# A transformer layer in float32 on one core: the down projection's first activations loaded in two turns, more weight sums made ahead, and matmuls of ones at the start

## The chip, the core and the metric

The kernel runs on one core of one Trainium2 chip. A core has five engines that follow their own instruction streams in order and wait for one another through semaphores: TensorE (PE, matrix products into PSUM banks), VectorE (DVE), ScalarE (ACT), GpSimd (POOL) and SyncE (SP). Tiles lie in SBUF with 128 partitions. DMA transfers are issued by SP, ACT or POOL and carried by 16 DMA engines.

The metric is the device time of one execution in microseconds (us).

## What is computed

One layer of an encoder for 512 tokens of width 2048, in float32. Cut to what matters:

```python
h  = rmsnorm(x, norm_mix)
qa, ka, va, qb, kb, vb, ga, gb = split(h @ w_in)        # 2048 x 8704
A  = window_attention(rope(rmsnorm(qa)), rope(rmsnorm(ka)), va, sink)   # 8 heads
B  = neighbourhood_attention(rmsnorm(qb), rmsnorm(kb), vb, rpb)         # 8 heads
merged = sigmoid(ga) * (A @ w_branch_a) + sigmoid(gb) * (B @ w_branch_b)
x  = x + merged @ w_out
h2 = rmsnorm(x, norm_ffn)
u  = depthwise_conv3(h2 @ w_up)                         # 2048 x 11264
gate, val = split(u)
x  = x + (silu(gate) * val) @ w_down                    # 5632 x 2048
```

## The kernel before

**Number format.** Activations are kept transposed (features on partitions, tokens in the free dimension). Every float32 operand is split in two halves of the rounded format fp32r, a high half by a cast on ACT and a low half by a subtraction on DVE, and every product is three matmuls: high by high, high by low, low by high. In the attention stage and the first gates the weights are split at L163 (`hi`) and L164 (`lo`); later at L645 (`wh`) and L646 (`wl`), or at L746 and L747 for weights that are multiplied as they are. Everything on PE is issued at L78.

**Stages.** First the projections of q, k and v with the heads of both attentions. The work of the heads is cut in pieces that wait in `queue`; each weight unit takes some of them along (`run_queued`, with raised priority). Where nothing is said to the contrary a scheduler sorts the instructions by a simulated timeline of its own; what is issued through `keep` or `dma` keeps the order of the program on its engine. Then the gates: `gates(0)` and `gates(4)` are two blocks of 512 columns in plain products (8 units of 1024x128 weights each, 96 matmuls of 128x512, 4 banks); at their end `gate_to_slot` multiplies the four banks on DVE (L848), applies the sigmoid on ACT (L849) and stores on POOL's queue (L854). The banks tagged `mm` are four, so the next block starts when L848 has emptied them. `gates(8)` ends the attention, and it loads x again and forms h for what follows. The heads that are still queued run beside the first gates: scores into `tr` banks, bias and mask on DVE (L531, L534), maximum (L477), exponential and scaling on ACT (L494), transposes on PE (L503), their split on ACT (L507) and DVE (L508), products with v on PE, and a copy of the output on ACT (L519).

**Products by sums.** From gate block 3 on a unit of weights is a 2x2 arrangement of blocks and is multiplied by seven products instead of eight, which needs sums of the weights' blocks (three DVE instructions for each unit, L600, L603, L604) and sums of the activations' blocks (`forms`). `combine` joins the seven banks (first an ACT copy, L799). The sums of some units are `kept`: made far ahead by `make_early`, while the unit counter `u` lies in one of the `windows`. For each such unit POOL loads two tiles of 256 KB (L614, `s<-in_w_up`), DVE adds four times one unit later (L620), and ACT's queue stores two tiles of 256 KB (`sums<-s`, L629) two units after that. When the unit's turn comes, SP loads one tile of 512 KB (`f<-sums`) in the place of one of 128 KB and the three sums. SBUF has 56 tiles of 128x512, `slot()`, for this and for all else.

**Down.** The 22 `up` steps leave `act` in DRAM: for each pair of 256 features eight blocks (four values and four sums, 128 KB each, seven blocks in the last part). `down(part, n)` multiplies three parts of 7, 7 and 8 pairs by four column blocks. `load_act` loads a pair's blocks on SP's queue, into one half of a slot each, and `split_act` splits them in place, each with an ACT cast (L1075) and a DVE subtraction (L1076) of 128x256. Part 0's pairs are loaded in the last `up` step and split from there on; those of parts 1 and 2 in the step ahead of their own. Steps (0,0), (0,3) and (1,3) use no sums: 48 matmuls of 128x256 a unit, of the four value blocks only (`tiles_by_halves`: tiles 0, 7, 1 and 6 of a pair). All other steps have 42 matmuls of 128x256 a unit.

**Start.** SP's queue loads `gmix` and then x and the first weights; POOL fills a tile `ones`, used at L276.

Of the kernel before, what the change touches and what calls it, by code (L numbers as in the profile page):

```python
# [11 lines left out]
F32 = mybir.dt.float32  # L12
F32R = mybir.dt.float32r
# [5 lines left out]
P = 128  # L19
# [20 lines left out]
def trunk_kernel(  # L40
# [6 lines left out]
    nc = tc.nc  # L47
# [32 lines left out]


    gmix = const.tile([P, KD], F32, tag="gmix", name="gmix")
    dma(gmix, norm_mix)
    warm = const.tile([P, 1], F32, tag="warm", name="warm")
    nc.vector.memset(warm, 0.0)
    nc.scalar.activation(warm, warm, AF.Square)
    ident = const.tile([P, P], F32, tag="ident", name="ident")
    make_identity(nc, ident)
    mhalf = const.tile([P, 16], F32, tag="mhalf", name="mhalf")
    nc.gpsimd.memset(mhalf, -0.5)  # L90
    ones = const.tile([P, P], F32, tag="ones", name="ones")
    nc.gpsimd.memset(ones, 1.0)
    nsink = const.tile([P, 8], F32, tag="nsink", name="nsink")
    n_kept = sum(width for _, width in KEPT)
    smalls = const.tile([P, n_kept], F32, tag="smalls", name="smalls")
# [473 lines left out]


    ffn, early, fetched, added, windows = {}, deque(), deque(), deque(), []
    keep = tc.keep_in_program_order

    class Product:

# [389 lines left out]
        nc.vector.tensor_tensor(r, r, s, ALU.add)  # L965
        merged[m] = split(r)

    windows.append((9, len(units)))
    for blk in range(2):
        gates(blk * 4, gate_to_slot)  # L970
    gates(8, gate_to_quad, pre=pre_forms, before=before_forms, post=post_forms)
    for blk in range(3, 8):
        gate_products(
# [85 lines left out]
    wait = lambda: None  # L1059
    unfinished = deque([wait, wait, wait])  # L1060

    def load_act(part, n):

        if 0 <= n < len(parts[part]):
            blocks = (0, 2, 7, 5, 4, 6, 3, 1)[:8 - (part == 2)]
            tiles = [slot(F32R) for _ in blocks]
            for o, i in zip(tiles, blocks):
                dma(o[:, 256:].bitcast(F32), act[parts[part][n]][:, i])
            acts[part].append(tiles)

    def split_act(part, n):
        if 0 <= n < len(parts[part]):
            for o in acts[part][n]:
                hi, lo = o[:, :256], o[:, 256:]
                keep(nc.scalar.copy(hi, lo.bitcast(F32)))  # L1075
                keep(nc.vector.tensor_tensor(  # L1076
                    lo, lo.bitcast(F32), hi.bitcast(F32), ALU.subtract))

    def up(s):
        def evac(gate, val):  # L1080
            g, v = Conv(gate, 2 * s), Conv(val, 44 + 2 * s)
            made = []

            def silu():
                keep(nc.scalar.activation(g.o, g.o, AF.Silu))

            def out_part():
                keep(nc.vector.tensor_tensor(v.o, g.o, v.o, ALU.mult))
                made.extend(form_sums(v.o))
# [12 lines left out]
        def before(i):  # L1102
            if s == 0 and i in (0, 2, 4):
                form_pair(5 + i // 2)
            if s == 0 and i == 4:
                rows["f"] = row_factor("f")
            if s == 0 and i == 7:
                rows["f"] = rows["f"]()[1]
            if s == pairs_ff - 1:
                load_act(0, i - 1)  # L1110

        def after(i):
            if s == pairs_ff - 1:
                split_act(0, i - 6)

        view = w_up.rearrange("(d b p) (h n) -> d p b h n", b=2, p=P, h=2)
        products(view[:, :, :, :, s * 256:(s + 1) * 256], range(KD // 2), h2, evac,
                 before=before, after=after, kept=(2, 3, 7) if s else range(8))

    def down(part, n):  # L1120
        held = []

        def before(i):
            if n == 0 and part:
                load_act(part, 6 + i)
            if part == n == 0 and i == 4:
                run_queued(1)
            if part == 0 and n == 1 and i == 1:
                queue.extend(unfinished)
            if part < 2 and n == 3:  # L1130
                load_act(part + 1, i - 1)
            if part == 2 and i == 4:
                for j in range(2):
                    held.append(quad("ao"[j]))
                    dma(held[j], total[2 * n + j])

        def after(i):
            if n == 0:
                split_act(part, i + (5 if part else 2))
            if part < 2 and n == 3:  # L1140
                split_act(part + 1, i - 2)

# [19 lines left out]
        else:  # L1162
            view = w_down.rearrange("(d b p) (s h n) -> s d p b h n", b=2, p=P, s=4, h=2)
            products(view[n], parts[part], acts[part], evac if part < 2 else evac_total,
                     before=before, after=after, kept=(0, 1) if part and n == 0 else (),
                     total=held if part == 2 else None)

    for s in range(pairs_ff):
# [70 lines left out]
```

## Time and profile before

| | |
|---|---|
| median of 3 executions | 2466.04 us (2465.09 to 2468.15) |
| the profiled execution | 2465.89 us |
| its span, first to last instruction | 2464.1 us |
| mean granted TensorE clock | 0.998 |
| PE, busy share of the span | 99% |
| DVE | 77% |
| ACT | 52% |
| POOL | 13% |

The chain of work that ended last lies with PE for 94% of the span, DVE 2%, DMA 1%, ACT 1%. Times below are us from the start of the span. A row of the timeline has the start, the length, the engine, the line, the operation, output<-input, the shape and the number of instructions, and in brackets the idle time before it with what ended it. A row of the windows has the stretch, its length, and for PE, PEld (weight load), DVE, ACT and POOL the busy us and the number of instructions, then the granted clock of PE, the busy share of the DMA engines and GB/s.

### The profile page before, as it was taken

The page shows a single profiled execution, that of the slowest core. Times are in us where ns is not written, and L with a number is a line of the kernel's source. Part 1 is how long each engine was busy: PE and PEld are TensorE (multiplying, and loading weights), DVE is VectorE, ACT ScalarE, POOL GpSimd, SP SyncE. Part 2 cuts the span into 40 slices and gives each one's busy share as a digit, 9 for nine tenths or more (in the row PEclk, how much of TensorE's full clock was granted, in tenths as well). Part 3 has the DMA queues.
Part 4 walks back from the last instruction along what each step waited for, and adds up shares of the span by engine and source line. Part 5 has one row for each costly group of instructions (what it writes and reads, how often), then busy time and mean ns, then how long its engine had stood idle before and what let it go on. Part 6 is the DMA issues. An engine that isn't in the chain of part 4 may idle for free.

```text
span 2464.1 us, 45745 instructions
## 1 busy us (share of the span) xinstructions
PE 2436.6 (99%) x17430; PEld 2276.2 (92%) x17430; DVE 1899.6 (77%) x3003; ACT 1283.5 (52%) x1962; POOL 330.5 (13%) x406
## 2 busy tenths in 40 slices
PE   9999999999999999999999999999999999999998
PEld 7888888888999888888999999999999999999998
DVE  6787667655888656557888888888888878696898
ACT  5354554365644322334666666666666666453633
POOL 1322122301000111111011111110111101000000
PEclk9999999999999999999999999999999999999999
DMA  5766766746655677777588888888888897766754
GB/s 197 257 230 213 234 207 230 238 139 205 197 163 175 200 271 245 237 232 245 166 213 230 224 225 224 218 234 222 224 228 218 234 277 187 218 187 176 221 158 131
DMA packets 340700, 525.45 MB, mean 213 GB/s; under 512 B 30720, under 2 KB 234112, under 8 KB 340480
## 3 DMA queue, kind: packets, MB, share of 16 engines
q1 hardware_dynamic: 254656, 319.68, 41.8%
q0 software_dynamic: 48384, 128.91, 21.8%
q10 hardware_dynamic: 37440, 73.94, 7.8%
q8 instruction: 136, 2.23, 0.4%
q14 instruction: 84, 0.69, 0.1%
HBM read 377.80 MB, written 98.57 MB: 193 GB/s over the span
## 4 chain that ended last, share of the span: by engine, by line
PE 94%; DVE 2%; DMA 1%; ACT 1%; issue 1%; SPq 0%; DVEq 0%; ACTq 0%
PE mm L78 91%; PE tr L78 2%; PE tr L503 1%; PE tr L351 0%; DVE wl L646 0%; DVE s L1076 0%; DMA a<-in_x_t 0%; DMA s<-act 0%; DMA f<-in_w_down 0%; ACT wh L645 0%; DVE u L795 0%; DVE s L687 0%; ACT s L1075 0%; DMA sums<-s 0%; DVE s L620 0%
## 5 line engine op out<-in xcount | busy, mean ns | idle before, releaser
L78 PE MATMUL mm<-s,wh 128*128 128x256 f32 (+1 forms) x9620 | 1725.0, 289 | 6.6 <-ACT wh L645 2.5
L78 PEld LDWEIGHTS mm<-s,wh 128*128 128x128 f32 x9620 | 1437.1, 188 | 48.7 <-ACT wh L645 3.1
L78 PE MATMUL mm<-s,wl 128*128 128x256 f32 (+1 forms) x4810 | 1249.9, 289 | 3.5 <-DVE wl L646 3.5
L78 PEld LDWEIGHTS mm<-s,wl 128*128 128x128 f32 x4810 | 851.0, 188 | 24.7 <-DVE wl L646 4.5
L645 ACT CAST wh<-f 128x1024 fp32r<-128x1024 f32 (+1 forms) x566 | 516.9, 942 | 482.5 <-PE mm L78 331.3
L646 DVE TENSOR_TENSOR wl<-f,wh 128x1024 fp32r<-128x1024 f32 (+1 forms) x566 | 601.8, 1088 | 147.7 <-ACT wh L645 146.3
L78 PE MATMUL mm<-hi,s 128*128 128x512 f32 x896 | 284.9, 394 | 5.7 <-ACT hi L163 5.7
L747 DVE TENSOR_TENSOR wl<-f,wh 128x1024 fp32r<-128x1024 f32 x85 | 104.1, 1224 | 165.4 <-ACT wh L746 159.7
L746 ACT CAST wh<-f 128x1024 fp32r<-128x1024 f32 x85 | 89.4, 1052 | 238.8 <-PE mm L78 207.0
L78 PEld LDWEIGHTS mm<-hi,s 128*128 128x128 f32 x896 | 167.6, 189 | 38.4 <-ACT hi L163 5.7
L163 ACT CAST hi<-raw 128x1024 fp32r<-128x1024 f32 (+1 forms) x97 | 100.9, 1040 | 188.5 <-PE mm L78 153.9
L78 PE MATMUL mm<-s,hi 128*128 128x512 f32 x640 | 195.4, 392 | 2.1 <-ACT o L519 1.6
L164 DVE TENSOR_TENSOR lo<-raw,hi 128x1024 fp32r<-128x1024 f32 (+1 forms) x97 | 117.5, 1211 | 102.8 <-ACT hi L163 98.7
L78 PE MATMUL mm<-lo,s 128*128 128x512 f32 x448 | 176.3, 395 | 0.0
L78 PEld LDWEIGHTS mm<-s,hi 128*128 128x128 f32 x640 | 119.2, 188 | 25.9 <-ACT o L519 1.8
L600 DVE TENSOR_TENSOR f<-f 128x512 f32<-128x512 f32 x195 | 133.5, 685 | 0.0
L1045 POOL DMA_DIRECT2D o<-a x44 | 52.9, 1202 | 557.8 <-ACT a L1044 336.9
L78 PE MATMUL mm<-s,lo 128*128 128x512 f32 x320 | 118.8, 391 | 0.0
L620 DVE TENSOR_TENSOR s<-s 128x256 f32<-128x256 f32 x236 | 93.2, 419 | 17.1 <-DMA s<-in_w_up 15.0
L78 PEld LDWEIGHTS mm<-lo,s 128*128 128x128 f32 x448 | 84.4, 188 | 16.6
L1042 ACT ACTIVATE o<-u,smalls 128x512 f32<-128x512 f32 x88 | 71.2, 809 | 33.3 <-DVE t L677 30.1
L603 DVE TENSOR_TENSOR f<-f 128x256 f32<-128x256 f32 x195 | 83.0, 426 | 6.7
(150 smaller groups left out, 2029.5 us busy)
## 6 DMA issues: line engine op xcount, KB each, us to landing
f<-sums SPq DMA_DIRECT2D x88, 512.0 KB, 5.3
f<-in_w_up SPq DMA_DIRECT2D x176, 256.0 KB, 3.8
o<-a POOLq DMA_DIRECT2D x88, 511.0 KB, 7.4
f<-in_w_up SPq DMA_DIRECT2D x281, 128.0 KB, 3.8
raw<-in_w_in SPq DMA_DIRECT2D x63, 512.0 KB, 4.4
sums<-s ACTq DMA_DIRECT2D x118, 256.0 KB, 4.1
s<-in_w_up POOLq DMA_DIRECT2D x86, 256.0 KB, 5.4
s<-act SPq DMA_DIRECT2D x168, 128.0 KB, 4.2
```

The lines of the kernel that those rows point to most:

```text
L78: return nc.tensor.matmul(o, l, r, start=start, stop=stop, skip_group_check=True).ins
L163: nc.scalar.copy(hi[:, c:c + n], self.raw[:, c:c + n])
L164: nc.vector.tensor_tensor(lo[:, c:c + n], self.raw[:, c:c + n], hi[:, c:c + n].bitcast(F32), ALU.subtract)
L600: keep(nc.vector.tensor_tensor(f[:, 3:5], f[:, 2::-2], f[:, 6].unsqueeze(1).to_broadcast([P, 2, 256]), ALU.add))
L603: keep(nc.vector.tensor_tensor(f[:, 5], f[:, 4], f[:, 2], ALU.add))
L620: add = lambda *args: keep(nc.vector.tensor_tensor(*args, ALU.add))
L645: keep(nc.scalar.copy(hi, f))
L646: keep(nc.vector.tensor_tensor(lo, f, hi.bitcast(F32), ALU.subtract))
L746: keep(nc.scalar.copy(hi, self.f))
L747: keep(nc.vector.tensor_tensor(lo, self.f, hi.bitcast(F32), ALU.subtract))
L1042: keep(nc.scalar.activation(self.o[:, m], u[:, m], AF.Identity, bias=cb[:, i:i + 1], scale=cw[:, i, 1:2]))
L1045: keep(nc.gpsimd.dma_start(self.o[:, :, 1:], first[:, :, :S - 1], accum_op=ALU.add))
```

## The change

Four edits:

1. At the start `gmix` is loaded on ACT's queue, `ones` is filled on DVE, and ten matmuls of ones by ones (128x128, float32) go to a bank that nobody reads.
2. The first window for early sums ends at `gates(8)` and no longer at `gates(0)`: it is 16 units longer.
3. `load_act` and `split_act` take a list of blocks. Part 0's values are loaded and split in the last `up` step and the beginning of (0,0), its sums in (0,0), and they are split there and in (0,1).
4. At (1,0) and (2,0) units 0 to 4 have kept sums in the place of units 0 and 1.

```diff
-    dma(gmix, norm_mix)
+    keep = tc.keep_in_program_order
+    keep(nc.scalar.dma_start(gmix, norm_mix))
...
+    ones = const.tile([P, P], F32, tag="ones", name="ones")
+    nc.vector.memset(ones, 1.0)
+    busy = bank("tr")
+    for _ in range(10):
+        keep(nc.tensor.matmul(busy[:, :P], ones, ones, start=True, stop=True))
...
-    windows.append((9, len(units)))
     for blk in range(2):
         gates(blk * 4, gate_to_slot)
+    windows.append((9, len(units)))
...
-    def load_act(part, n):
+    BLOCKS, VALUES, SUMS = (0, 2, 7, 5, 4, 6, 3, 1), (0, 1, 6, 7), (2, 3, 4, 5)
+
+    def load_act(part, n, which=None):
         if 0 <= n < len(parts[part]):
...
+            if n == len(acts[part]):
+                acts[part].append([None] * 8)
+            for i in which or range(8 - (part == 2)):
+                acts[part][n][i] = slot(F32R)
+                dma(acts[part][n][i][:, 256:].bitcast(F32), act[parts[part][n]][:, BLOCKS[i]])
...
             if s == pairs_ff - 1:
-                load_act(0, i - 1)
+                load_act(0, i - 2, VALUES)
...
             if s == pairs_ff - 1:
-                split_act(0, i - 6)
+                split_act(0, i - 6, VALUES)
...
             if n == 0 and part:
                 load_act(part, 6 + i)
+            if part == n == 0:
+                load_act(0, 6 + i, VALUES)
+                load_act(0, i, SUMS)
...
-            if n == 0:
-                split_act(part, i + (5 if part else 2))
+            if n == 0 and part:
+                split_act(part, i + 5)
+            if part == n == 0:
+                split_act(0, i + 2, VALUES)
+                split_act(0, i - 2, SUMS)
+            if part == 0 and n == 1:
+                split_act(0, i + 5, SUMS)
...
-                     before=before, after=after, kept=(0, 1) if part and n == 0 else (),
+                     before=before, after=after, kept=range(5) if part and n == 0 else (),
```

In number: 97 units are kept after the change, 91 before. Of the 91 the windows had room for 88, among them of the down units only unit 0 of (1,0). The first window now makes 75 units' sums in the place of 59, the second 22 in the place of 29, and all 97 are made.

**PE between the first two blocks of gates.** A row is a line and an operation with output<-input and shape, "x" the number in a row. `mm` are the banks of the gates (and `s,hi` and `s,lo` their operands), `tr` those of the heads: `tr<-s` are scores, `tr<-ident,p` transposes, `tr<-ph,s` and `tr<-pl,s` products with v. Before, in the middle of the second block:

```order
L78 MATMUL mm<-s,hi 128x512 x2
L78 MATMUL tr<-ph,s 128x256
L78 MATMUL mm<-s,lo 128x512
L78 MATMUL mm<-s,hi 128x512
L78 MATMUL tr<-s 128x256 x6
L78 MATMUL tr<-pl,s 128x256
L78 MATMUL tr<-ph,s 128x256 x2
L78 MATMUL tr<-pl,s 128x256
L78 MATMUL tr<-ph,s 128x256
L78 MATMUL mm<-s,hi 128x512
L78 MATMUL mm<-s,lo 128x512
```

After the change, from the last matmul of the first block:

```order
L78 MATMUL mm<-s,lo 128x512
L78 MATMUL tr<-s 128x256 x12
L507 MATMUL tr<-ident,p 128x128 x2
L78 MATMUL tr<-ph,s 128x2x128
L507 MATMUL tr<-ident,p 128x128 x4
L78 MATMUL tr<-pl,s 128x2x128
L78 MATMUL tr<-ph,s 128x2x128
L78 MATMUL tr<-ph,s 128x256
L507 MATMUL tr<-ident,p 128x128 x2
L78 MATMUL tr<-s 128x256 x3
```

The rows after these go on in the same way: 84 instructions of the heads (56 matmuls 256 wide and 28 transposes; line numbers are 3 to 5 higher in the changed kernel) stand in one piece between the two blocks, with no `mm` among them; before they stood inside the second block, between its matmuls.

**DVE at the same place.** Here L848 (L851 after the change) empties the four banks of the first block. L531, L534, L477 and L508 are steps of the heads, L240 one of an earlier head, L164 a split of weights. Before:

```order
L240 SCALAR_TENSOR_TENSOR s<-tr,masks,s 128x512 x2
L164 TENSOR_TENSOR lo<-raw,hi 128x1024
L240 SCALAR_TENSOR_TENSOR s<-tr,masks,s 128x512 x2
L848 TENSOR_TENSOR s<-mm,row 128x512 x4
L531 SCALAR_TENSOR_TENSOR p<-tr,bias 128x192
L531 SCALAR_TENSOR_TENSOR p<-tr,bias 128x256 x2
L164 TENSOR_TENSOR lo<-raw,hi 128x1024
L534 TENSOR_TENSOR p<-p,masks 128x192
```

After (L623 are the early adds, L620 before):

```order
L512 TENSOR_TENSOR pl<-tr,ph 128x256
L623 TENSOR_TENSOR s<-s 128x256 x2
L512 TENSOR_TENSOR pl<-tr,ph 128x256 x2
L623 TENSOR_TENSOR s<-s 128x256
L512 TENSOR_TENSOR pl<-tr,ph 128x256
L623 TENSOR_TENSOR s<-s 128x256
L851 TENSOR_TENSOR s<-mm,row 128x512 x4
L623 TENSOR_TENSOR s<-s 128x256 x2
L168 TENSOR_TENSOR lo<-raw,hi 128x1024
```

The four instructions that empty the banks stood ahead of the two heads' work; now they stand behind all of it: 8 of L535 (bias), 8 of L538 (mask), 8 of L481 (maximum), 12 of L512, 2 small ones and 18 early adds come between the last earlier head and L851.

**SP's queue from the last up step to down.** `act_169` and so on are the pairs of part 0 (`act_180` and so on after the change), `f<-in_w_down` the weights of (0,0). Before:

```order
L75 DMA f<-in_w_up 128x256 x2
L75 DMA s<-act_169 128x256 x8
L75 DMA f<-in_w_up 128x2x256
L75 DMA f<-in_w_up 128x256 x2
L75 DMA s<-act_170 128x256 x8
L75 DMA f<-in_w_up 128x2x256
L75 DMA f<-in_w_up 128x256
L75 DMA f<-sums_261 128x1024
L75 DMA s<-act_171 128x256 x8
L75 DMA f<-in_w_down 128x2x512
L75 DMA s<-act_172 128x256 x8
```

After:

```order
L75 DMA f<-in_w_up 128x256 x2
L75 DMA s<-act_180 128x256 x4
L75 DMA f<-in_w_up 128x2x256
L75 DMA f<-in_w_up 128x256
L75 DMA f<-sums_272 128x1024
L75 DMA s<-act_181 128x256 x4
L75 DMA f<-in_w_down 128x2x512
L75 DMA s<-act_182 128x256 x4
L75 DMA f<-in_w_down 128x2x512
L75 DMA s<-act_183 128x256 x4
L75 DMA f<-in_w_down 128x2x512
```

Ahead of the first weights of down stood the blocks of three pairs, 24 transfers; now the values of two pairs stand there, 8 transfers. The sums of part 0 follow later, inside (0,0).

More of the change, by code (lines that the diff above doesn't have):

```diff
@@ L90, in trunk_kernel @@
     nc.gpsimd.memset(mhalf, -0.5)
-    ones = const.tile([P, P], F32, tag="ones", name="ones")
-    nc.gpsimd.memset(ones, 1.0)
     nsink = const.tile([P, 8], F32, tag="nsink", name="nsink")
@@ L571, in trunk_kernel @@
     ffn, early, fetched, added, windows = {}, deque(), deque(), deque(), []
-    keep = tc.keep_in_program_order
     class Product:
@@ L1060, in trunk_kernel, with split_act @@
     unfinished = deque([wait, wait, wait])
-    def load_act(part, n):
+    BLOCKS, VALUES, SUMS = (0, 2, 7, 5, 4, 6, 3, 1), (0, 1, 6, 7), (2, 3, 4, 5)
+    def load_act(part, n, which=None):
         if 0 <= n < len(parts[part]):
[L1065 to L1071, printed above, removed]
+            if n == len(acts[part]):
[3 more added lines that the diff above has]
+                dma(acts[part][n][i][:, 256:].bitcast(F32), act[parts[part][n]][:, BLOCKS[i]])
+    def split_act(part, n, which=None):
         if 0 <= n < len(parts[part]):
-            for o in acts[part][n]:
+            for i in which or range(8 - (part == 2)):
+                o = acts[part][n][i]
                 hi, lo = o[:, :256], o[:, 256:]
```

## The prediction

> **What bounds the kernel now.** I read the page first (busy times), then PE's waits with their releasers, then the timeline and the windows at the places where those waits lie.
>
> ```profile
> PE 2436.6 (99%) x17430; PEld 2276.2 (92%) x17430; DVE 1899.6 (77%) x3003; ACT 1283.5 (52%) x1962; POOL 330.5 (13%) x406
> ```
>
> PE is busy for 2436.6 of 2464.1 us. The change leaves the number of products as it is, so it can only touch 27.5 us of idle time, and stretches in which PE runs slowly. From the end it can lose without limit. All times are of the profiled execution, 2465.89 us, which lies 0.15 below the median of the runs shown, 2466.04; I predict against the former. A measurement of this kernel can tell about 0.2% from no change, that is 4.9 us, so "same" means 2461.1 to 2471.0.
>
> **The change part by part: the start.** The rows are the first issues on SP's queue, the first products on PE, and the split of the third unit of weights.
>
> ```profile
> 0.74 0.39 SPq L75 DMA_DIRECT2D gmix<-in_norm_mix  x1
> 5.70 2.08 PE L78 MATMUL mm<-hi,s 128*128 128x512 f32 x4 [5.70 <-ACT hi L163]
> 8.43 0.55 PE L78 MATMUL mm<-lo,s 128*128 128x512 f32 x1
> 8.81 0.40 PE L78 MATMUL mm<-hi,s 128*128 128x512 f32 x1
> 9.05 0.39 PE L78 MATMUL mm<-lo,s 128*128 128x512 f32 x1
> 14.55 1.05 ACT L163 CAST hi<-raw 128x1024 fp32r<-128x1024 f32 x1 [0.20 <-DMA raw<-in_w_in]
> 16.19 1.22 DVE L164 TENSOR_TENSOR lo<-raw,hi 128x1024 fp32r<-128x1024 f32 x1
> ...
> L276 PE MATMUL tr<-t,ones x8: 272/275/275, 51.7 to 52.5; 128*128 128x128 f32 x8
> ```
>
> Without `gmix` x is issued about 0.45 earlier. From 5.70 to 8.81 PE starts seven matmuls, 0.44 apart; from 8.81 to 9.05 the step is 0.24. Seven at 0.23 would take 1.6, so 1.5 us go to a slow start. The row of `ones` shows float32 products in two passes each (four instructions, eight records in 0.8 us, 0.1 each); ten of them are 20 passes, 2 us at that pace and 4 to 5 at half of it. Issued from about 1.2 they end at 3.2 to 6, so they cover most of the wait before the first weights, or come 0.5 too late. But the third unit's weights come by DMA at 14.55 and their low halves are made up to 17.4, about when PE wants them now: what PE gains before that it partly waits there. Bounds −2.0 (0.45 and 1.5) and +0.5; I take **−0.9**, since the row at 14.55 shows a DMA as the limit behind it.
>
> **From up to down.** Windows, SP's issues, and the waits.
>
> ```profile
> 2005.00:2010.00 5.00, 3.36 (x23) 2.55 (x21) 3.83 (x9) 4.51 (x11) 1.20 (x1) 1.00 1.09 315
> 2010.00:2015.00 5.00, 3.11 (x17) 2.92 (x18) 2.59 (x4) 3.50 (x8) 0.00 (x0) 0.74 1.07 264
> 2015.00:2020.00 5.00, 5.00 (x28) 5.00 (x28) 4.69 (x10) 1.45 (x5) 0.00 (x0) 0.58 0.82 272
> 2020.00:2025.00 5.00, 5.00 (x46) 5.00 (x45) 4.89 (x11) 4.46 (x10) 0.00 (x0) 1.00 0.84 275
> ...
> 1995.88 9.41 SPq L75 DMA_DIRECT2D s<-act  x8
> 2005.39 0.45 SPq L75 DMA_DIRECT2D f<-in_w_down  x1
> 2004.78 1.05 ACT L746 CAST wh<-f 128x1024 fp32r<-128x1024 f32 x1 [4.64 <-DMA f<-in_w_down]
> 2009.56 0.38 PE L78 MATMUL mm<-s,wh 128*128 128x256 f32 x1 [1.18 <-ACT s L1075]
> 2013.09 0.80 PE L78 MATMUL mm<-s,wh 128*128 128x256 f32 x2 [1.66 <-ACT t L799]
> 2007.39 2.77 DVE L1076 TENSOR_TENSOR s<-s 128x256 fp32r<-128x256 f32 x8 [0.30 <-ACT s L1075]
> ```
>
> In 15 us from 2005 there are 23+17+28 = 68 matmuls; at 46 in 5 us (0.109 each) there would be 138. The products of both steps are 128x256 at this pace, so the lack of 70 matmuls is 70 × 0.109 = 7.6 us: some 3 in visible waits, the rest in the clock of 0.74 and 0.58 that follows them. The cause is the queue: eight loads of `act` held SP for 9.41, and the next weights of down were issued behind them, so ACT waited 4.64 for weights and split activations behind that. The change puts 8 transfers ahead of the first weights where 24 stood, and 16 in the place of 32 splits per four units. The sums go behind, into (0,0), where nothing needs them until (0,1). The splits left (four, half of 2.77 us on DVE) are spread over a unit. I take **−7.5**; the bounds are −7.8 (all of it, and the odd wait) and −3.0 (the visible waits go, 1.66, 1.18 and smaller ones, and the clock falls all the same).
>
> **Heads of down's parts 1 and 2.**
>
> ```profile
> PE mm L78 <- DVE wl L646: 3.5, 4, 1.1
> ...
> 2181.27 0.39 PE L78 MATMUL mm<-s,wl 128*128 128x256 f32 x1 [1.15 <-DVE wl L646]
> 2351.60 1.88 PE L78 MATMUL mm<-s,wh 128*128 128x256 f32 x14 [1.25 <-ACT wh L645]
> 2320.00:2330.00 10.00, 8.58 (x73) 8.30 (x73) 9.54 (x18) 3.84 (x5) 0.00 (x0) 1.00 0.62 179
> ...
> L600 DVE TENSOR_TENSOR f<-f 128x512 f32<-128x512 f32 x66 | 45.2, 685 | 0.0
> L603 DVE TENSOR_TENSOR f<-f 128x256 f32<-128x256 f32 x66 | 28.1, 426 | 2.3
> L604 DVE TENSOR_TENSOR f<-f 128x256 f32<-128x256 f32 x66 | 28.1, 425 | 2.3
> ```
>
> All four waits for DVE's `wl` (3.5 us) and the one of 1.25 at 2351 lie in the first units of these steps: 4.75 together. DVE is at 9.54 of 10 there: it makes the sums (0.69+0.43+0.43 = 1.54 a unit), the low halves, and the splits of the pairs still to come (seven or eight at 2.77/8 = 0.35) inside a unit of some 42 × 0.109 = 4.6 us. Kept sums take 1.54 away in four more units of part 1 and five of part 2 — a third of a unit, and more than any of the waits. They add 384 KB to each of these units' loads; the DMA share in the window is 0.62, which leaves room, though it can rise past what SP's order allows. I take **−4.5**; bounds −4.75 and 0 (a wait for `f<-sums` in the place of that for DVE).
>
> **The window by the gates.** This is the largest term, and it comes from the place of the heads and of L851 in the two orders shown, not from the additions themselves. The durations:
>
> ```profile
> L531 DVE SCALAR_TENSOR_TENSOR p<-tr,bias 128x256 f32<-128x256 f32 x7 | 2.8, 418 | 2.8 <-PE tr L78 2.8
> L477 DVE TENSOR_REDUCE nm<-p 128x1 f32<-128x192 f32 x8 | 2.7, 342 | 0.0
> L508 DVE TENSOR_TENSOR pl<-tr,ph 128x256 fp32r<-128x256 f32 x20 | 8.0, 419 | 7.1 <-ACT ph L507 7.0
> L848 DVE TENSOR_TENSOR s<-mm,row 128x512 f32<-128x512 f32 x8 | 5.4, 688 | 3.1 <-PE mm L78 3.1
> L494 ACT ACTIVATE p<-p,rc 128x256 f32<-128x256 f32 x4 | 1.8, 495 | 0.0
> L519 ACT COPY o<-tr 128x512 f32<-128x512 f32 x5 | 5.5, 1090 | 2.1 <-PE tr L78 2.1
> ...
> 495.28 0.60 PE L503 MATMUL tr<-ident,p 128*128 128x128 f32 x4
> 579.72 0.73 PE L78 MATMUL mm<-s,hi 128*128 128x512 f32 x2 [1.63 <-ACT o L519]
> ...
> 580.00:585.00 5.00, 5.00 (x23) 4.12 (x23) 0.00 (x0) 0.09 (x1) 2.00 (x3) 1.00 0.86 243
> ```
>
> After the first block PE has the heads' 84 instructions and no gate matmul: 56 × 0.109 + 28 × 0.125 (four transposes in 0.60, their last end taken off) = 9.6 us of work. The second block can only start when L851 has emptied a bank, and L851 now stands behind 56 DVE instructions: 46 of 0.35 (the spacing in the row of eight in 2.77), eight maxima of 0.34, two small ones, 19 us in all. With L851's 0.69 PE goes on 19.7 after the end of the block if DVE never waits. It will wait: in the trace DVE idled 7.0 us at 20 of L508's instructions for ACT's `ph`, 0.35 each, 4.2 for twelve; and ACT has scalings of 0.5 and copies of 1.09 between. L531 and L508 last 0.42 each, spaced 0.35. Following the three engines row by row I come to 3.2 of waits, 22.9 in all. PE is idle for 22.9 − 9.6 = 13.3, and the only wait that the same heads gave before, 1.63 at 579.72, goes: **+11.7**, with bounds of +8.5 (no DVE wait) and +12.7 (all 4.2).
>
> Two smaller things follow. The third unit of the second block needs its cast on ACT, which stands behind the scaling of the first x, whose load stands on POOL's queue behind three stores of gates. PE has two units ready, 24 × 0.23 each, 11 us. L848, the sigmoid, the store, and a load like those below lead to about the same: **+0.5**, from 0 to 3.4. And after such idle time the clock was at 0.58 in the window of 2015, where 18 matmuls or 2.0 us were lost, with some in the slice ahead: **+2.5**, from 0 to 5. The gates thus cost +14.7. The 16 early units themselves (four adds, 1.4 us a unit of 5.5, on a DVE that is 77% busy) I count as nothing beside this; without the heads in one piece they would hide behind PE.
>
> The Trainium skill, "TensorE: Matmul & The Clock Gate", section "What's actually happening", says that the clock halves after at least one idle window of about 3.4 us. The trace speaks against a strict reading: the clock row falls to 0.74 and 0.58 after gaps of no more than 1.66. By the page PE's pieces of work between the gaps would keep the clock, and the sum would be 2.5 lower.
>
> **The rivals.** *The clock holds*: PE works on pieces of two to twelve matmuls between the gaps; if these keep it at full speed, as the clock stayed at 1.00 from 580 to 585, right after the 1.63, the sum is 2.5 lower, 2465.2. *The adds are late as well* (slower): the early adds ahead of L851 wait for their loads, and the loads for slots that only stores set free; ACT issues these stores among the heads' steps.
>
> ```profile
> POOL s L614 <- DMA sums<-s: 35.1, 9, 9.2
> ...
> s<-in_w_up POOLq DMA_DIRECT2D x28, 256.0 KB, 5.7
> sums<-s ACTq DMA_DIRECT2D x27, 256.0 KB, 4.1
> ```
>
> A store that ACT issues some 17 us into the heads, its 4.1 and the next load's 5.7 bring the last adds to 27 where I have 22.2, so L851 4.8 later, and the clock stays low for 2.5 longer: 2475.0. It decides from the point at which a slot's way of 9.8 us is longer than what is left of the heads. For it: POOL's loads already wait for stores, nine times and up to 9.2. Against: the fetch is a unit ahead, and 56 slots are not all in use here. *Down is not cured*: the four loads still meet `o<-a` accumulations and weights on the DMA engines, whose share is 1.09 at 2005; only 3 of 7.5 come: 2472.2. *The heads cost only DVE's bare work* (faster): DVE never waits and the clock and the third unit cost nothing, +8.5, and the other terms come at their full bounds, −7.8 −4.75 −2.0: 2465.89 − 6.05 = 2459.8. That the early sums are not made at all is excluded: the order has their adds.
>
> **How the numbers follow.** −0.9 − 7.5 − 4.5 + 14.7 = +1.8, so 2465.89 + 1.8 = **2467.7**. Chances: forecast 0.38, clock held (2465.2) 0.10, adds late (2475.0) 0.22, down not cured (2472.2) 0.12, bare work (2459.8) 0.18. Same holds forecast and clock, 0.48; slower 0.34; faster 0.18. The ends of the terms would reach further in both directions, but not all at once; from a little under the fast case to a little over the slowest, 2459 to 2477, at most 2 in 10 are left out.
>
> **What would show it.** In the changed profile: PE idle for some 13 us between the first two blocks of gates, put down to DVE or ACT's `ph`, and a lower clock behind it; if PE is idle for under 6 there, the largest term is wrong. Around 2005 to 2020 no clock under 0.9, 46 matmuls in 5 us, and no wait over 0.3 for L1075 or the weights; else the queue was not the cause. No wait for `wl` in the first units of parts 1 and 2; if one for `f<-sums` stands there, DMA took DVE's place. At the start a spacing of 0.23 from the first product on, and a wait before 18; without the wait I have undervalued the ones. What would make the whole wrong is a gates' order that DVE passes through much faster than by single durations.

## The result and the profile after

The changed kernel takes 2490.33 us (median of 4, 2489.23 to 2493.78), the kernel before on the same chip 2467.1 (4 runs): a ratio of 1.0097, 95% interval 1.008 to 1.0115. That is 23 us slower, outside the predicted range of 2459 to 2477. The profiled execution is 2489.23 us long with a span of 2487.3 (2465.89 and 2464.1 before).

The page and PE's waits after the change (line, output, engine and line waited for: us in total, times, longest):

```profile
PE 2447.7 (98%) x17450; PEld 2284.2 (92%) x17450; DVE 1899.4 (76%) x3013; ACT 1280.8 (51%) x1960; POOL 342.8 (14%) x423
...
PE 90%; DMA 4%; DVE 2%; issue 2%; ACT 1%; SPq 0%; POOL 0%; ACTq 0%; DVEq 0%; POOLq 0%
```

```profile
PE tr L78 <- ACT s L243: 8.0, 1, 8.0
PE mm L78 <- ACT wh L648: 6.8, 5, 2.5
PE tr L78 <- ACT ph L511: 4.4, 7, 1.1
PE mm L78 <- ACT s L1082: 2.7, 1, 2.7
PE mm L78 <- ACT hi L167: 2.5, 2, 1.4
```

Idle time of PE rose from 27.5 to 39.6 us, and PE is busy 11 us longer: 4.6 of it are the ten products of ones; the rest I put down to products that run slower behind its waits, where the granted clock is lower (windows below). On the chain that ended last DMA has 4% in the place of 1%.

**Where the time went.** Both kernels run the same 16,734 products into `mm` banks. Numbered in order of their start, the same product can be compared in two traces. This table gives how many us later (or, with a minus, earlier) it starts than in the kernel before, at seven numbers; the second row is where that product lies in the trace of before. It holds the experiments too.

```
product                      40    3000   12900   12960   13600   14500   16733
start before, us           16.3   704.3  2005.6  2020.1  2094.1  2198.1  2456.8
changed kernel             -0.9    23.2    24.9    17.1    22.0    23.1    22.8
e1  window back            -0.9     1.8     2.2    -5.6    -0.9    -0.9    -0.8
e2  window alone            0.7    22.3    22.3    22.9    22.8    23.0    23.2
e4  turns alone             0.1    -0.4    -0.5    -8.2    -4.9    -4.8    -4.7
e5  half window            -2.1    12.7    13.8     6.2    10.3    11.4     9.9
e6  pad elsewhere          -2.0    27.5    27.9    20.7    27.3    27.3    25.8
e8  gates' own tiles       -1.6    23.0    24.2    16.4    21.6    25.1    23.9
e9  turns, store on POOL   -0.1    -0.7    -0.7    -8.2    -7.9    -7.8    -7.8
e10 start, turns, store    -1.4    -0.9    -0.7    -8.5    -8.0    -7.9    -7.8
e11 half rate              -1.0     9.1     9.2     1.4     7.9    11.1     9.8
e12 two slots              -0.9    -4.1    -3.4   -10.2    -4.8    -3.3    -4.6
e13 two slots, store       -2.2    -3.6    -2.0    -9.1    -8.8    -4.3    -5.9
e14 and one kept at (1,0)  -1.9    -4.0    -2.8   -10.1    -9.7    -9.6   -11.5
```

Read along the row of the changed kernel: 0.9 won at the start; 24.1 lost by product 3000, all between 490 and 660 us; 7.8 won in the first stall of down (12900 to 12960); 4.9 lost again within the next 75 us, 1.2 of it within ten products of number 12960 and most of the rest in a second stall; then 1.1 lost at the head of part 1 and 0.3 won to the end.

**The gates.** Windows of the changed kernel (columns as before), then rows of its timeline on PE, ACT, DVE and POOL:

```profile
525.00:530.00 5.00, 0.00 (x0) 0.00 (x0) 3.72 (x8) 1.75 (x3) 1.36 (x2) 0.95 1.03 363
530.00:535.00 5.00, 2.08 (x8) 1.79 (x9) 4.54 (x11) 1.51 (x3) 0.26 (x2) 0.50 1.04 386
...
550.00:555.00 5.00, 3.59 (x15) 3.33 (x16) 2.51 (x7) 2.33 (x6) 0.00 (x0) 0.50 0.58 226
```

```profile
532.92 3.29 PE L78 MATMUL tr<-s 128*128 128x256 f32 x12 [8.05 <-ACT s L243]
...
524.68 1.04 ACT L167 CAST hi<-raw 128x1024 fp32r<-128x1024 f32 x1 [5.28 <-PE mm L78]
524.74 4.19 ACTq L632 DMA_DIRECT2D sums<-s  x3
528.98 0.69 ACT L243 ACTIVATE s<-tr,masks 128x512 fp32r<-128x512 f32 x1 [3.25 <-DVE s L623]
...
525.76 1.22 DVE L168 TENSOR_TENSOR lo<-raw,hi 128x1024 fp32r<-128x1024 f32 x1 [3.50 <-ACT hi L167]
526.90 2.34 DVE L623 TENSOR_TENSOR s<-s 128x256 f32<-128x256 f32 x6
555.90 2.48 DVE L851 TENSOR_TENSOR s<-mm,row 128x512 f32<-128x512 f32 x4
```

The first block of gates ends at about 524.9. PE's next work are the scores of the last heads, and their operands are not there: 8.05 us of waiting that I had not foreseen. The rows show why. ACT's cast of the next weights waits for PE (until 524.68), DVE's subtraction for the cast, six early adds stand behind it, three stores on ACT's queue wait for adds, and L243, which makes the operands, stands behind these stores. In the kernel before the same steps (L239 there) were done while PE still worked:

```profile
514.06 0.69 ACT L239 ACTIVATE s<-tr,masks 128x512 fp32r<-128x512 f32 x1
518.91 1.26 ACT L239 ACTIVATE s<-tr,masks 128x512 fp32r<-128x512 f32 x2
```

From the scores at 532.92 to L851 at 555.90 it is 23.0, where I had forecast 22.2; the piece of 84 instructions and L851 behind it are as predicted.

**Down.** PE's, DVE's and ACT's rows in (0,0) and the windows around them:

```profile
2038.72 0.38 PE L78 MATMUL mm<-s,wh 128*128 128x256 f32 x1 [0.90 <-DVE s L1083]
...
2048.61 0.42 DVE L680 TENSOR_TENSOR t<-t,o 128x256 f32<-128x256 f32 x1
2053.31 1.15 ACTq L1101 DMA_DIRECT2D act<-t  x2
2054.52 0.81 ACT L1045 ACTIVATE o<-u,smalls 128x512 f32<-128x512 f32 x1 [4.08 <-DMA f<-in_w_down]
...
2057.61 0.85 PE L78 MATMUL mm<-s,wh 128*128 128x256 f32 x5 [2.70 <-ACT s L1082]
...
2030.00:2035.00 5.00, 5.00 (x47) 5.00 (x46) 3.93 (x8) 5.00 (x13) 1.20 (x1) 1.00 1.09 296
2055.00:2060.00 5.00, 2.39 (x15) 2.40 (x16) 2.42 (x8) 5.00 (x13) 1.20 (x1) 0.87 0.93 306
2060.00:2065.00 5.00, 5.00 (x37) 5.00 (x37) 2.96 (x8) 5.00 (x11) 1.20 (x1) 0.79 1.03 240
```

The stall from up to down is gone but for one wait: 47 matmuls stand in the 5 us from 2030 at full clock, and then PE waits 0.90 for a subtraction of `split_act` (L1083). The prediction had asked for no wait over 0.3 for L1075's casts or the weights, and named no wait for the subtraction. From 2055 on 52 matmuls stand in 10 us where 94 would, 4.6 us at 0.109. ACT stood for 4.08 at its stores of the last but one pair of `act`; the release that the profile names is a DMA that SP issued, weights of down. What the stores write was made by 2049.03 (the last step is DVE's L680), so it is not DVE that held them. Behind these stores stand four convolution steps and the casts (L1082) for which PE waits.

**The heads of parts 1 and 2.** PE, ACT and SP at (1,0), then PE in (2,0):

```profile
2202.87 1.40 PE L78 MATMUL mm<-s,wh 128*128 128x256 f32 x10 [2.49 <-ACT wh L648]
2198.96 2.31 ACT L1082 CAST s<-s 128x256 fp32r<-128x256 f32 x7 [3.88 <-DMA s<-act]
2187.90 10.29 SPq L75 DMA_DIRECT2D s<-act  x8
...
2367.46 0.39 PE L78 MATMUL mm<-s,wl 128*128 128x256 f32 x1 [0.91 <-DVE wl L649]
2374.04 1.92 PE L78 MATMUL mm<-s,wh 128*128 128x256 f32 x14 [1.25 <-ACT wh L648]
```

The wait for DVE at (1,0), 1.15 before, has become one of 2.49 for ACT, which waits for the last blocks of `act`. In (2,0) the last two waits are what they were (0.92 and 1.25): they lie in units behind the five that are kept.

### The profile page after: what moved, and what is told of

It is laid out like the page before. It is cut to its first block, busy times and chain, and to the rows that moved or that the text cites. A ratio compares the mean times of both kernels' runs of the same rounds, so it can differ in the third digit from the quotient of the medians.

```text
span 2487.3 us, 45875 instructions
## 1 busy us (share of the span) xinstructions
PE 2447.7 (98%) x17450; PEld 2284.2 (92%) x17450; DVE 1899.4 (76%) x3013; ACT 1280.8 (51%) x1960; POOL 342.8 (14%) x423
## 4 chain that ended last, share of the span: by engine, by line
PE 90%; DMA 4%; DVE 2%; issue 2%; ACT 1%; SPq 0%; POOL 0%; ACTq 0%; DVEq 0%; POOLq 0%
PE mm L78 87%; DMA s<-act 2%; PE tr L78 2%; DMA f<-in_w_down 1%; DMA a<-in_x_t 1%; DVE wl L649 1%; PE tr L507 0%; PE tr L355 0%; DVE u L798 0%; SPq L75 0%; DVE s L1083 0%; DMA raw<-in_w_in 0%; DMA s<-out_a 0%; ACT wh L648 0%; PE tr L92 0%
## 5 line engine op out<-in xcount | busy, mean ns | idle before, releaser
L623 DVE TENSOR_TENSOR s<-s 128x256 f32<-128x256 f32 x300 | 118.0, 418 | 15.6 <-DMA s<-in_w_up 12.8
L603 DVE TENSOR_TENSOR f<-f 128x512 f32<-128x512 f32 x186 | 127.2, 684 | 0.0
L617 POOL DMA_DIRECT2D s<-in_w_up x118 | 85.3, 725 | 86.3 <-DVE s L623 28.2
```

The lines of the kernel that those rows point to most:

```text
L603: keep(nc.vector.tensor_tensor(f[:, 3:5], f[:, 2::-2], f[:, 6].unsqueeze(1).to_broadcast([P, 2, 256]), ALU.add))
L617: keep(nc.gpsimd.dma_start(x, self.w[:, :, h]))
L623: add = lambda *args: keep(nc.vector.tensor_tensor(*args, ALU.add))
```

## The experiments

The theory at the start: the window makes the loss (by the heads in one piece and L851 behind them), and the turns give part of their gain back. Rivals: another edit is behind the loss at the gates; or it is not the order of instructions but the early loads or the slots that they hold. All ratios are to the kernel before on the same chip.

**The window put back, and the window alone.** The first restores this in the changed kernel, the second makes the opposite edit in the kernel before:

```diff
-    for blk in range(2):
-        gates(blk * 4, gate_to_slot)
     windows.append((9, len(units)))
+    for blk in range(2):
+        gates(blk * 4, gate_to_slot)
```

> The changed kernel with the first window ending at gates(0) again; the start, the turns of the activations and kept=range(5) stay, but the windows then have room for 88 sums, so units 1 to 4 of (1,0) and all of (2,0) get none. Theory (the window costs what the gates lose, 23.9 us by comparing the start of the same matmul in both traces): those 23.9 come back, -0.9 at the start and about -3.0 from up to down remain, 2463.5, and PE has no wait over 2 us between 500 and 600. Rival (the early loads only uncover a stall that another edit causes, the moved memset or gmix load ahead of it): the gates stay slow, over 2480.

> The kernel before with the longer first window and nothing else. Theory: the same 24 us at the gates, 2491 (down's kept units 0 and 1 change it by under 1.5). Rival (several edits together make the loss): under 2480.

Back: 2464.17 us, ratio 0.9998 (0.9989 to 1.0008). Alone: 2489.22, 1.0097 (1.0082 to 1.0112), with the same wait of 8.05 on PE. Up to product 3000 the window alone loses 21.6 of the changed kernel's 24.1, and without it 2.7 are lost: the window is the loss, and the other edits have no large part in it. Most of the 2.7 stand at the first products of the third block. The kernel of e10, with the window put back too, loses 0.5; what makes the difference is not known.

**The turns alone**, in the kernel before:

> The kernel before with the loads of part 0's activations in two turns and nothing else. Theory (the first stall goes, 7.2 us, and 4.2 of it come back some 40 us later, where ACT's stores of act stand behind the loads of the sums): 2467.1 - 3.0 = 2464.1, with a wait for L1075's casts of 2 to 3 us in (0,0). Rival (the second stall comes from the other edits, which shift what is in flight): 2459.9, with no such wait.

2463.77 us, 0.9992 (0.9983 to 1.0001). The trace: 7.7 us won, 3.3 given back with a wait of 1.78 for the casts. Start, window and kept sums are not needed for the second stall.

**Half of the window**: `windows.append` between `gates(0)` and `gates(4)`.

> The changed kernel with the first window ending at gates(4): half of the 16 additional units. In its order of instructions the heads do not stand in one piece between the first two blocks of gates (no run of 84). Theory A (the order in one piece, with L851 behind it, makes the loss): the gates lose under 3 us against the kernel with the window at gates(0). Theory B (the early loads themselves make it, by slots and DMA, in proportion to their number): about 12 us are lost there. Theory C (slots that the last heads' operands wait for, the 8 us wait at L243): 6 to 10 are lost, as a wait of PE for the operands of the scores at the end of the first block.

2479.71 us, 1.0063 (1.0046 to 1.008); in the trace 14.8 us are lost to product 3000. The scores wait 8.05 here too, to the hundredth as in the changed kernel, in e2 and in e6. A wait that is the same whenever loads land points to a fixed chain of instructions from the end of the block, as the rows above show it. Theory A, that the piece and L851 are all of it, falls, since no piece of 84 stands here; C and B are left.

**The padding on DVE**: `nc.vector.memset` in the place of `nc.gpsimd.memset` at L484.

> The changed kernel with the memset of the heads' padding (L484) on DVE in the place of POOL. In the changed kernel POOL's memset at 508.07 waited 10.45 us for the heads' transposes, the early loads queued behind it left as a burst of eight, and the DMA share was 1.03 to 1.04 from 510 to 535. Theory (late loads hold the adds on DVE, the adds hold the stores on ACT's queue, and these hold ACT's L243, for which PE waits 8.05): the loads leave in time, that wait falls under 3 us, the kernel gains 5 to 8, 2482 to 2485. Rival (the loads wait for free slots anyway): 2489 to 2491, and the wait stays at 8.

2493.76 us, 1.0115 (1.0101 to 1.0129). The wait is 8.05 again, and ahead of it PE waits 4.96 for a cast (at 501.86) where it waited 1.42. The loads do not leave in time here either: a pair at 530.61 waits 10.33 for a store of sums. So the run shows that the memset is not the cause, as the rival has it; what earlier loads would do it doesn't show.

**The gates' outputs in tiles of their own.**

```diff
     def gate_to_slot(m, ps):
-        s = slot()
+        s = scratch()
```

> The changed kernel with the outputs of the first two blocks of gates in the four scratch tiles and not in slots. Loads, adds and stores of the early sums stay all 16 units, but in the order of instructions the heads no longer stand in one piece between the blocks and L851 stands among them. Theory A (order): the loss at the gates falls to what the half window kept, 12 to 14 of 24, so 2478 to 2480; the 8 us wait for L243 stays. Theory B (the number of early loads, adds and stores): the loss stays over 20, 2487 or more. Theory C (slots alone, with the outputs of the gates as their missing share): the wait for L243 goes too, loss under 5, 2471 or less.

2489.64 us, 1.0102 (1.0088 to 1.0116): nothing is won, against theories A and C. But the loss has moved. L851 stands among the heads and the second block is 6 us ahead of before at 548. Then 29 instructions of the heads stand in one piece at the end of the second block, PE waits for them (2.49 at 576) and is 8.6 behind before; and it waits at the first products of the third block. The rows are the last store of the heads' output, the loads of x and that wait, and then the first two of them in the kernel before:

```profile
588.34 0.33 ACTq L527 DMA_DIRECT2D out_b<-o  x1
594.22 1.44 POOL L868 DMA_DIRECT2D a<-in_x_t  x2 [10.30 <-DMA sums<-s]
654.42 1.86 PE L78 MATMUL mm<-s,wh 128*128 128x256 f32 x7 [10.02 <-ACT wh L648]
...
579.70 0.33 ACTq L523 DMA_DIRECT2D out_b<-o  x1
582.64 1.45 POOL L865 DMA_DIRECT2D a<-in_x_t  x2 [1.71 <-DMA out_b<-o]
```

From these loads of x the forms of h are made. Their tile is no slot: it lies in space that the heads' tiles leave when the attention ends. In the kernel before they are released by the last store of the heads' output. Here that store is issued 8.6 later and by the trace's semaphores landed at 593.56, just before the loads; the store of sums that the bracket names is a false trail. So the loss has moved to the heads' late end and to what waits for it. The run shows that the piece of 84 is not needed for a loss of this size. It does not show that the order has no part, because the heads are late by the order here too.

**Half the rate** on the 16 units: a load only in every second one.

```diff
-        if early and any(a <= u < b - 4 for a, b in windows) and not (wide and u % 2):
+        if early and any(a <= u < b - 4 for a, b in windows) and not (
+                (wide or u >= windows[0][1] - 20) and u % 2):
```

> The changed kernel with the additional stretch of the window at half the rate: a load for an early sum in every second of the 16 units, so 8 of them. In its order the heads still stand in one piece of 62 between the blocks of gates. Theory (slots: an early unit holds three of the 56 for some three units, the loads and the heads' and gates' outputs wait for one another, and the order puts heads and L851 behind; half the rate asks for half the slots): the loss at the gates falls from 24 to 8 or less, 2475. Rival 1 (order alone, by the piece that is left): 18 to 22 remain, 2485 to 2489. Rival 2 (in proportion to the early units, as 8 of them in the first half cost 13): 12 to 13, 2479.

2473.81 us, 1.0034 (1.0022 to 1.0047); 10.1 us lost to product 3000. The 8 us wait is 1.50 here, but a piece of 62 is left. It lies between the theory's 8 and the 12 of proportion, and tells these two apart only weakly. (The theory's three slots for some three units are too many, as the next run shows.)

**Two slots for an early sum.** The four adds work in place, so the third tile goes; the loads, the number of adds and the bytes stored stay:

```diff
             a, b = self.early
-            c = quad("o")[:, 0] if "q" in ffn else slot()
+            if "q" not in ffn:
+                add(a[:, 0], a[:, 0], b[:, 0])
+                add(b[:, 0], b[:, 1], b[:, 0])
+                add(b[:, 1], a[:, 0], b[:, 1])
+                add(a[:, 1], b[:, 1], a[:, 1])
+                self.early = b, a
+                return
+            c = quad("o")[:, 0]
...
-                keep(nc.scalar.dma_start(self.kept[:, 2 * i:2 * i + 2], o))
+                at = slice(2 * i, 2 * i + 2) if "q" in ffn else slice(i, None, 2)
+                keep(nc.scalar.dma_start(self.kept[:, at], o))
```

> The changed kernel with the early adds made in place: an early sum holds two slots and not three, with the same loads, the same four adds and two stores of 256 KB (each a stride of two blocks in DRAM in the place of two neighbours). In its order no piece of the heads stands between the blocks of gates any more. Theory (slots): the loss at the gates falls from 24 to under 6, with the DMA share there still near 1; 2466 to 2472. Rival (bandwidth, DVE or the queues, whose work is the same): the loss stays over 18, 2484 or more, or moves to the third block as in the kernel with the gates' own tiles.

2463.07 us, 0.9985 (0.9976 to 0.9993). Product 3000 starts 4.1 us earlier than before, not 23.2 later; even the waits that the kernel before had at 497 to 511 are gone. Windows of this kernel, for the stretch in which the changed kernel stood still:

```profile
520.00:530.00 10.00, 9.84 (x54) 8.31 (x54) 6.93 (x18) 6.59 (x13) 1.41 (x3) 1.00 0.80 283
530.00:540.00 10.00, 10.00 (x53) 8.45 (x52) 8.54 (x24) 7.80 (x16) 5.98 (x10) 1.00 0.97 305
540.00:550.00 10.00, 10.00 (x51) 8.41 (x50) 5.84 (x12) 3.10 (x5) 0.00 (x0) 1.00 0.99 352
```

PE works throughout, with a DMA share up to 0.99 and all 16 units' sums made. So bandwidth and DVE's adds are no limit here: with the same loads, adds and stores, the loss hangs on the third slot. The operands of the last heads are made at 492 to 498 (L243), 22 us earlier than in the kernel before.

That is not the same as fewer slots held. With three tiles, one is held from the load to the add one unit later, one from the load to the store (three units) and one from the add to the store (two), six in tiles times units. With two tiles, both are held for three units, which is six as well. Worked out from the traces (POOL's loads, DVE's adds, the landing of the stores), the early sums hold 7.5 slots on average between 440 and 560 us in the changed kernel and 8.1 in this one. POOL's early loads wait about as long (31.7 and 34.1 us from 440 to 660). What goes away is that an add must be given a free slot. In the changed kernel the adds show only one wait from 440 to 660, 1.6 us for a load and none for a store. That speaks for the order, which the scheduler draws up from its own simulated waits for slots, and in which the heads come so much earlier here. The runs do not separate the order from the waits on the chip, for in-place adds change both.

One number puts the runs nearly in order: when ACT starts the last of the heads' operands. It is 498 us in e12, 519 in the kernel before, 526 in e11, 532 in e5, 533 in the changed kernel and e2, 538 in e6 and 541 in e8. From product 40 to 3000 these kernels lose −3.2, 0, 10.1, 14.8, 24.1 and 21.6, 29.5 and 24.6. This goes with the late operands, but is no proof that they are the cause in each run.

**The store of `act` on POOL's queue**, alone with the turns (e9), then with the changed start (e10):

```diff
-                    keep(nc.scalar.dma_start(act[s][:, o:o + x.shape[1]], x))
+                    keep((nc.gpsimd if s == pairs_ff - 2 else nc.scalar).dma_start(
+                        act[s][:, o:o + x.shape[1]], x))
```

> The two turns alone, with the store of the last but one pair of act on POOL's queue and not on ACT's. Theory (ACT's stores wait for a DMA that is issued on SP's queue among the loads of the sums, and hold ACT's casts behind them): the wait of 1.8 to 2.7 us for L1082's casts in (0,0) and the slow clock behind it go, 2 to 4 us better than the turns alone, 2460 to 2462. Rival (ACT is late by its own work, conv and splits together): the wait stays, within 1 us of the turns alone.

> The changed start, the two turns and the store on POOL's queue; the window and the kept units as before. Theory (the terms add: -0.9 at the start, -7 from up to down): 2465.9 - 8 = 2458, faster than both kernels, ratio 0.9965 to 0.997. Rival (the start's gain is taken back, as the third unit's weights come by DMA): 1 us more.

2458.77 us, 0.9975 (0.9965 to 0.9986), and 2459.74, 0.9975 (0.9967 to 0.9984). Against the turns alone e9 wins 5.0 in the medians and 3.1 in the traces (−7.8 against −4.7), where 2 to 4 were expected. The first row below is of the turns alone, the second of e9: the same ACT step comes 3.2 us earlier when no store stands ahead of it. (DVE's row, which the former names, is not what held it: in e9 the step starts without it.) The window shows no second stall.

```profile
2028.35 0.81 ACT L1042 ACTIVATE o<-u,smalls 128x512 f32<-128x512 f32 x1 [3.15 <-DVE u L1029]
...
2025.15 0.81 ACT L1042 ACTIVATE o<-u,smalls 128x512 f32<-128x512 f32 x1
...
2030.00:2035.00 5.00, 5.00 (x47) 5.00 (x46) 2.95 (x7) 5.00 (x11) 0.76 (x1) 1.00 1.05 228
```

The rival (ACT too busy by its own work) falls: ACT is busy all the time here and PE doesn't wait. The start adds nothing that these runs can show, since e10's 2459.74 is not below e9's 2458.77, though its trace is 1.4 ahead at product 40: by product 3000 it is level (−0.9 against −0.7). That is nearer to the rival than to the sum of the terms.

**All four edits without the two faults**, then the kept sums of (1,0) back to unit 0:

> The same with the store of the last but one pair of act on POOL's queue: all four edits of the change, without the two faults that the runs have shown. Theory (slots and ACT's store are the two causes, and the terms add): 4 us better than the two slots alone. If early sums then cost nothing, 2459 or less, as with the window left as it was (2459.7), and the heads of down's parts bring at most 1 more; if they still cost some, that much more.

```diff
-                     before=before, after=after, kept=range(5) if part and n == 0 else (),
+                     before=before, after=after, kept=((), (0,), range(5))[part] if n == 0 else (),
```

> The kernel with two slots and the store on POOL's queue, with units 0 to 4 of (2,0) kept and of (1,0) unit 0 alone, as before the change. Theory (at (1,0) the kept units' 384 KB more a unit lie on DMA engines with a share of 1.05, and the splits wait for the last act blocks: PE waits 3.06 there, where 1.13 was waited for DVE without kept sums; at (2,0) the kept sums take 0.59 + 0.82 of waits away): the wait at (1,0) goes back to about 1.1, 2 us better than with both, 2457.4. Rival (the 3 us come from elsewhere, such as the order of SP's queue by the turns): the wait stays, 2459.

2459.42 us, 0.997 (0.9958 to 0.9982), and 2454.0, 0.995 (0.9936 to 0.9964). The wait at (1,0), of the former and of the latter:

```profile
2172.67 3.36 PE L78 MATMUL mm<-s,wh 128*128 128x256 f32 x14 [3.06 <-ACT wh L657]
...
2171.70 0.39 PE L78 MATMUL mm<-s,wl 128*128 128x256 f32 x1 [1.15 <-DVE wl L658]
```

Four units fewer with `f<-sums` there, and the wait for `act` is gone. The first is as expected (3.7 under the two slots alone). The two were measured on different chips; they lie 6.7 and 11.6 us under the kernel before on the same chip, so 4.9 apart where 2 were expected. Their traces differ by 5.6 at the end: 0.9 stood already at 2094, 4.4 come at (1,0), with what follows the wait there, and 0.3 later. e14 is faster than both kernels.

## Why the prediction was wrong, by its steps

- **The gates, +14.7 forecast, +24.1 measured.** The mechanism named for the changed kernel (the heads in one piece, L851 behind them) stood in its trace as forecast, 23.0 us from the scores to L851 where 22.2 were worked out. What failed is the step before it: I let the heads start when the block ended. Their operands came 8.05 later, since L243 stands behind a cast that waits for PE's block, behind adds and behind stores on ACT's queue. I had followed PE's and DVE's order from the end of the block on, but not ACT's order ahead of the scores. Of the smaller terms, the cast for the third unit of the second block cost 1.10 (at 568.97) where I put 0.5, and a like wait of 1.42 at 499.48, ahead of the end of the first block, I did not have at all.
- **Its cause: the window is shown, what works inside it is open.** I argued from the order, called the 16 early units nothing beside it, and said that they would hide behind PE without the heads in one piece. That does not hold: e8 has no piece of 84 and loses as much, e5 has none either and loses 14.8. e12 shows that the loss hangs on the third slot of an early sum, and not on its loads, adds and stores. Whether that slot works through the order, as I had argued, or through waits on the chip stays open. The rival "the adds are late as well" had the slots in it, but only as an addition of 4.8 behind the piece; what came was a wait ahead of it.
- **The clock fell**, 0.50 in two windows of the gates, as I had it, against the rival that it holds. At 550 to 555 it is 0.50, after 1.00 in the window before, with PE busy 3.59 of 5 us and no wait over 1.14 since 533. The Trainium skill, "TensorE: Matmul & The Clock Gate", section "What's actually happening", asks for an idle window of about 3.4 us: by a strict reading the clock should have stayed full there, and the trace does not agree. The 2.5 that I put for it are not to be found as a loss of their own: the piece took 0.8 more than was worked out without it, and the second block's products stand 0.23 apart from 557.26 on.
- **From up to down, −7.5 forecast: −7.8 measured, and 4.9 given back.** The −7.8 are read at the best point; a wait of 0.90 for a split stands right behind it. The term was right in the main; its bound was not, because I called the sums' loads harmless where nothing needs them. They were in the way of something else: ACT's stores, which wait for a DMA of SP's queue and hold ACT. e9 shows it.
- **The heads, −4.5 forecast, +0.8 measured.** (From 1.1 lost and 0.3 won.) Two errors: two of the five waits, 2.17 of 4.75, lie in units that are not kept, which the numbers of the units would have told me; and at (1,0) the added loads, which I allowed for only as a bound, make a longer wait than DVE did, as e14 shows.
- **The start, −0.9 forecast, −0.9 measured**, and luck has a part in it:

```profile
1.09 4.63 PE L92 MATMUL tr<-ones 128*128 128x128 f32 x20 [1.09 <-DVE ones L89]
4.28 0.60 ACT L167 CAST hi<-raw 128x512 fp32r<-128x512 f32 x1
5.38 2.02 PE L78 MATMUL mm<-hi,s 128*128 128x512 f32 x4
...
7.48 0.40 PE L78 MATMUL mm<-hi,s 128*128 128x512 f32 x1
7.71 0.39 PE L78 MATMUL mm<-lo,s 128*128 128x512 f32 x1
```

The first weights are cast by 4.88, but the ones run on and the first product starts at 5.38: they come half a us too late, which the prediction had as a bound, and still win. From the sixth product on the spacing is 0.23, where it was 0.44 up to 8.81 before. In the traces of the other kernels the same start gave 0.9 to 2.2 at product 40; by product 3000 of e10 it was no longer to be seen.

With the forecast's own sum: −0.9 − 7.5 − 4.5 + 14.7 = +1.8; the trace has −0.9 − 7.8 + 4.9 + 0.8 + 24.1 = +21.1, and 1.7 between products 3000 and 12900 make the +22.8 of the end.

## What to carry to other kernels

Work that is moved ahead needs a buffer at each of its steps, and a shared pool hands the bill to whoever allocates next. Ask of each step whether it can write in place, and try that first; counting tiles times units would not have found it here, since both versions come to six. When work is to begin at a certain point, follow the order of every engine that feeds it ahead of that point, and not only from there on. When one stall is taken out of a stage, look at every in-order queue that is fed from there, for a store that waits on one engine's queue stops the casts behind it. And when the order is cured without the time changing, look where the loss went, and check the releaser that the profile names against the tiles.

## What the runs showed of the hardware that I had not expected

The granted clock fell to 0.50 with waits of at most 1.14 us, when PE was busy for about 70% of the stretch (3.59 of 5 us). Ten float32 products of 128x128 showed as 20 records in 4.63 us and shortened the slow start of the products behind them, from seven products to four. A store on ACT's queue stood until a DMA issued on SP's queue had landed: two queues that exchange no data there were in step, for 4.08 us in the changed kernel. By the trace each of the three stores shares its semaphore of completion with a DMA of SP's (landed at 2052.60, 2053.24 and 2053.61), and each leaves within 0.13 us of that landing; with the stores on POOL's queue (e9) the wait is gone.
